# A 4096-cubed matmul with leaky ReLU: the first two output regions computed in three turns over k instead of one

## The chip, the core and the metric

The kernel runs on one core of a Trainium2 chip. The metric is the device time of one launch in microseconds (us). The core has a tensor engine (PE) for matmuls, a vector engine (DVE), a scalar engine (ACT), GpSimd (POOL) and a sync engine (SP). Each engine works through its own list of instructions in order and waits at an instruction until the semaphores that it needs have been raised. POOL and SP also issue DMAs, each into its own queue; both queues are served by the same 16 DMA engines.

## What is computed

```
x = np.matmul(a, b)                 # a, b: 4096 x 4096 fp32
return np.where(x > 0, x, alpha*x)  # alpha = 0.01
```

The products are made in bf16 with fp32 accumulation, so both inputs have to be rounded on the way in, and `a` has to be transposed, because the tensor engine wants k on the partitions for both operands.

## The kernel before

The output is cut into regions of 512 rows by 1024 columns (4 blocks of 128 rows, called mt, times 2 halves of 512 columns, called nt). One region fills all 8 PSUM banks, one bank for each (mt, nt). Two regions, h = 0 and h = 1, lie one under the other and share the same 1024 columns of `b`. The depth k = 4096 is cut into 4 units u of 1024, each of 8 chunks c of 128. A region is 4 x 8 x 4 x 2 = 256 matmuls of 128x128 by 128x512.

**A.** `load_a` (L71 to L85) brings 256 rows of `a` (index mp, two of them for 512 rows) over the k of one unit or half unit. Four DMAs, issued by POOL, read fp32 and write bf16 into an `a16` buffer (there are 4 of these); one DVE transpose (L83) of 32x32 blocks then writes the finished tile into `at`. A DMA on POOL's queue waits for the semaphore of the DMA eight before it, so eight can be under way.

**B.** `load_b` (L87 to L98) brings one chunk: one DMA of 512 KB issued by SP into a `b32` buffer (4 of these), and a cast to bf16 into `bt`, on ACT (L96) for the first 32 chunks and on DVE (L98) for all later ones. The `bt` pool has 6 buffers of one unit each.

**The first two regions** are written out by hand (L168 to L266), because nothing is in SBUF when they start. `subs` (L55) is the list of pieces of k: numbers 0 and 1 are the two halves of unit 0 (4 chunks each, "small"), numbers 2, 3 and 4 are units 1, 2 and 3 (8 chunks each, "large"). `TURNS` (L19) says which pieces are done together before the other region gets its turn. A step is one piece for one region. With one turn holding all five pieces the steps are h0 with pieces 0 to 4, then h1 with pieces 0 to 4: ten steps, numbered 0 to 9.

For each step, L175 to L188 list the loads: for h = 0 two A tiles mixed with the B chunks of the piece, for h = 1 the two A tiles alone, because B is then there already. The loads of step i+1 are put into the engines' lists by `ahead` (L235), in four quarters between the quarters of step i's matmuls. A step that is the last of its turn goes through its matmuls block by block (mt outside, c inside), and behind each block calls `spill(mt)` (L211) and then `ahead(mt)`. Other steps go chunk by chunk (c outside, mt inside). In the last turn `spill` also does the output: two leaky-ReLU instructions on ACT (L232) into an `o` buffer (2 of these) and one DMA to `out`, issued by POOL (L233). So on POOL's list the output DMA of block mt stands ahead of the A loads that `ahead(mt)` adds after it.

During steps 8 and 9 the kernel begins to load the B chunks of the next pair of regions (`issue`, L161; L255 and L263). From region 2 on, a plain loop (L269 to L293) does all 256 matmuls of a region and its output, and the loads are issued one or more units ahead.

Of the kernel before, what the change touches and what calls it, by code (L numbers as in the profile page):

```python
# [15 lines left out]

TURNS = [[0, 1, 2, 3, 4]]  # L19


@with_exitstack
def kernel(
# [76 lines left out]
    def mm(ps, mb, h, pi, u, mt, nt, c, first, last):  # L100
        nc.tensor.matmul(  # L101
            ps,
            at[mb, h, u][:, c, mt * P:(mt + 1) * P],
            bt[pi, u][:, c, nt * NT:(nt + 1) * NT],
            start=first,
            stop=last,
        )

    def new_banks():
        return {  # L110
            (mt, nt): psum_pool.tile([P, NT], FP32, name="ps")
            for mt in range(MT)
            for nt in range(NP)
        }
# [46 lines left out]
    def issue(slot, part):  # L161
# [7 lines left out]
        (t, h, sub, i == len(turn) - 1)  # L169
        for t, turn in enumerate(TURNS)  # L170
        for h in range(HALVES)
# [19 lines left out]
    part = {}  # L191
    if len(TURNS) > 1:
        for piece in queue[0]:
# [3 lines left out]
    for i, (t, h, si, last) in enumerate(steps):  # L197
# [4 lines left out]
        queue[i] = []  # L202
        if si == TURNS[t][0]:
            banks = new_banks()

        def go(mt, c):
            for nt in range(NP):
                mm(banks[mt, nt], 0, h, 0, u, mt, nt, c0 + c, si == TURNS[t][0] and c == 0,
                   last and c == kc - 1)

        def spill(mt):  # L211
            if not last:
                return
            for nt in range(NP):
                ps = banks[mt, nt]
                if len(TURNS) == 1:
                    continue
# [8 lines left out]
                else:  # L226
                    nc.vector.tensor_add(kept, ps, kept)
            if t == len(TURNS) - 1:
                o = o_pool.tile([P, RN], FP32, name="o")
# [99 lines left out]
```

## Time and profile before

| what | value |
|---|---|
| median of 3 runs | 1827.9 us (1827.43 to 1828.4) |
| the profiled execution | 1827.43 us, its span 1825.7 us |
| tensor engine | 8192 matmuls of the product, busy 97% of the span, mean granted clock 0.989 |
| 0 to 165 us (first two regions) | granted clock 0.88 between 12 and 165 us |
| 165 to 1825 us (the other 14) | granted clock 1.00, no idle time of the tensor engine recorded |
| queue of SP (B) | 220.23 MB |
| queue of POOL (A and most of the output) | 98.59 MB, counted as written |

The span is what the profile covers; the 1.7 us between it and the execution's time lie around it. Times inside the trace are counted from the span's start. A row of a timeline gives the start, the duration, the engine, the line and the operation, how many instructions were merged into the row, and in square brackets how long the engine was idle before it and what ended the wait. "DVE at L83" as a releaser means that the transpose of an A tile came last. Some matmul records are missing, so counts of matmuls in a row can be a little low, and the missing ones can be worked out from the order of the program.

### The profile page before, as it was taken

What the parts mean: (1) busy time and instruction counts of PE and PEld (TensorE: products, weight loads), DVE (VectorE), ACT (ScalarE), POOL (GpSimd) and SP (SyncE); (2) the same over time, 40 slices, a digit from 0 to 9 for tenths busy, and PEclk for the clock granted to TensorE, in tenths of its full rate; (3) what the DMA queues carried; (4) which work ended last, traced back from release to release, by engine and by line L of the source; (5) the groups of instructions that cost most, each with busy time, mean ns of one, the idle gap of its engine ahead of it and who ended that gap; (6) DMA issues with size and microseconds to landing.
All of it is one profiled execution on the core that took longest, in us unless ns stands there. A gap on an engine that the chain in (4) does not pass through costs nothing.

```text
span 1825.7 us, 18868 instructions
## 1 busy us (share of the span) xinstructions
PE 1776.4 (97%) x8041; PEld 804.5 (44%) x8204; DVE 475.6 (26%) x465; ACT 174.3 (10%) x290; POOL 253.6 (14%) x448
## 2 busy tenths in 40 slices
PE   5789999999999999999999999999999999999999
PEld 2334444444444444444444444444444444444444
DVE  1454231214442213022452312201255130311000
ACT  5200000000000000000000000000000000000001
POOL 3150000033310000003520000001242000000000
PEclk7899999999999999999999999999999999999999
DMA  9799773465585629155856835617387581644111
GB/s 325 181 162 352 270 272 143 181 141 101 100 235 210 230 105 338 65 196 81 131 100 230 289 126 198 263 64 226 62 111 198 203 337 46 244 171 160 70 46 47
DMA packets 166037, 320.04 MB, mean 175 GB/s; under 512 B 46657, under 2 KB 95809, under 8 KB 165953
## 3 DMA queue, kind: packets, MB, share of 16 engines
q1 hardware_dynamic: 61056, 220.23, 33.0%
q0 software_dynamic: 104896, 98.59, 24.7%
q8 instruction: 64, 1.05, 0.2%
q14 instruction: 21, 0.16, 0.0%
HBM read 285.21 MB, written 67.11 MB: 193 GB/s over the span
## 4 chain that ended last, share of the span: by engine, by line
PE 93%; DMA 4%; issue 2%; POOL 1%; DVE 0%; ACT 0%; POOLq 0%; DVEq 0%
PE ps L101 93%; DMA a<-in_a_dram 4%; POOL a L81 0%; POOL out_dram L233 0%; DVE at L83 0%; ACT o L288 0%; DVEq L83 0%; POOLq L81 0%; POOLq L233 0%; POOLq L310 0%
## 5 line engine op out<-in xcount | busy, mean ns | idle before, releaser
L101 PE MATMUL ps<-bt,at 128*128 128x512 bf16 x8029 | 1772.1, 381 | 43.4 <-DVE at L83 34.7
L101 PEld LDWEIGHTS <-at 128*128 128x128 bf16 x8192 | 803.0, 98 | 1012.5 <-DVE at L83 40.2
L98 DVE CAST bt<-b 128x1024 bf16<-128x1024 f32 x384 | 256.6, 691 | 851.9 <-PE ps L101 553.0
L83 DVE STREAM_TRANSPOSE at<-a 128x2048 bf16<-128x2048 bf16 (+1 forms) x80 | 219.4, 2779 | 365.1 <-DMA a<-in_a_dram 241.9
L288 ACT ACTIVATE o<-ps 128x512 f32<-128x512 f32 x240 | 130.7, 595 | 1524.1 <-PE ps L101 1408.2
L292 POOL DMA_DIRECT2D out_dram<-o x116 | 64.5, 556 | 1364.8 <-ACT o L288 1355.8
L81 POOL DMA_DIRECT2D a<-in_a_dram x320 | 183.4, 587 | 83.4 <-DMA a<-in_a_dram 50.5
L96 ACT CAST bt<-b 128x1024 bf16<-128x1024 f32 x32 | 33.4, 1045 | 26.1 <-DMA b<-in_b_dram 26.1
L232 ACT ACTIVATE o<-ps 128x512 f32<-128x512 f32 x16 | 8.7, 594 | 97.4 <-PE ps L101 87.9
L233 POOL DMA_DIRECT2D out_dram<-o x8 | 5.5, 687 | 66.5 <-ACT o L232 66.5
L126 PE MATMUL ps<-w 128*128 128x512 bf16 x12 | 4.3, 532 | 2.3 <-ACT w L123 2.3
L126 PEld LDWEIGHTS <-w 128*128 128x128 bf16 x12 | 1.5, 131 | 4.6 <-ACT w L123 2.3
L123 ACT ACT_TABLE_LOAD x1 | 1.3, 1283 | 0.7 <-PEq L310 0.7
L122 DVE MEMSET w<- 128x256 uint32 x1 | 0.3, 272 | 0.9 <-PEq L310 0.9
L123 ACT ACTIVATE w<-w 128x8 bf16<-128x8 bf16 x1 | 0.2, 208 | 0.0
L310 POOL MEMSET const-float32-0.0<- 128x1 f32 x1 | 0.1, 98 | 0.2 <-issue 0.2
L310 POOL MEMSET const-bfloat16-1.0<- 128x1 bf16 x1 | 0.1, 101 | 0.0
L310 POOL MEMSET const-float32-1.0<- 128x1 f32 x1 | 0.1, 98 | 0.0
L310 POOL MEMSET const-uint8-127<- 128x1 uint8 x1 | 0.1, 98 | 0.0
## 6 DMA issues: line engine op xcount, KB each, us to landing
b<-in_b_dram SPq DMA_DIRECT2D x416, 512.0 KB, 5.4
out_dram<-o POOLq DMA_DIRECT2D x124, 512.0 KB, 2.9
a<-in_a_dram POOLq DMA_DIRECT2D x192, 128.0 KB, 5.1
a<-in_a_dram POOLq DMA_DIRECT2D x128, 64.0 KB, 3.3
out_dram<-o SPq DMA_DIRECT2D x8, 256.0 KB, 2.0
```

The costliest lines, as they stand in the source:

```text
L81: nc.gpsimd.dma_start(a16[32 * q:32 * q + 32], src.rearrange("(g i) w -> i g w", i=32))
L83: nc.vector.transpose(dst.rearrange("p c (g i) -> p g c i", g=8), a16.rearrange("p g (j c) -> p g c j", c=kc))
L96: nc.scalar.copy(bt[pi, u][:, c0 + c, :], b32)
L98: nc.vector.tensor_copy(bt[pi, u][:, c0 + c, :], b32)
L101: nc.tensor.matmul(ps, at[mb, h, u][:, c, mt * P:(mt + 1) * P], bt[pi, u][:, c, nt * NT:(nt + 1) * NT], start=first, stop=last,)
L123: nc.scalar.activation(w[:, :8], w[:, :8], LRELU, alpha=alpha)
L126: nc.tensor.matmul(wp, w[:, :P], w, start=True, stop=True)
L232: nc.scalar.activation(o[:, nt * NT:(nt + 1) * NT], done, LRELU, alpha=alpha)
L233: nc.gpsimd.dma_start(place(0, h, pairs[0], mt), o)
L288: nc.scalar.activation(o[:, cols], banks[mt, nt], LRELU, alpha=alpha)
L292: nc.gpsimd.dma_start(to, o)
L310: nc = _bacc.Bacc("TRN2", target_bir_lowering=False, num_devices=1)
```

## The change

```
--- before
+++ after
-TURNS = [[0, 1, 2, 3, 4]]
+TURNS = [[0], [1, 2], [3, 4]]
```

The ten steps now are: 0: h0 piece 0; 1: h1 piece 0; 2 and 3: h0 pieces 1 and 2; 4 and 5: h1 pieces 1 and 2; 6 and 7: h0 pieces 3 and 4; 8 and 9: h1 pieces 3 and 4. Steps 0, 1, 3, 5, 7 and 9 are the last of their turn. At each of these all 8 PSUM banks are handed on, so `spill` has work to do, which it skipped with one turn:

```
for nt in range(NP):
    ...
    if h not in part:
        part[h] = bt_pool.tile([P, MT, NP, NT], FP32, name="part", tag="bt")
    kept = part[h][:, mt, nt, :]
    if t == 0:
        if h == 0 and nt:
            nc.vector.tensor_copy(kept, ps)
        else:
            nc.scalar.copy(kept, ps)
    else:
        nc.vector.tensor_add(kept, ps, kept)
if t == len(TURNS) - 1:
    o = o_pool.tile([P, RN], FP32, name="o")
    ...                                   # leaky ReLU now reads kept, not the bank
    nc.gpsimd.dma_start(place(0, h, pairs[0], mt), o)
```

The first turn copies 16 banks to SBUF (12 on ACT, 4 on DVE); the second and third turns add 16 banks each to what is kept there, on DVE; the leaky ReLU of the two regions reads the kept sums. The sums of a region take one buffer of the `bt` pool. The matmuls, their number, the bytes moved and everything from region 2 on stay as they are, apart from which `bt` buffer a unit gets.

## The prediction

> **What bounds the kernel now.** I read the busy shares in 40 slices first. From the fourth slice on PE is busy nine tenths or more at full clock; what can be moved lies in the first 165 us.
>
> ```profile
> PE   5789999999999999999999999999999999999999
> PEclk7899999999999999999999999999999999999999
> ```
>
> Next the timeline of PE in this stretch (the bracket is the wait ahead of the row), and the last of region 2 on ACT's timeline, which dates the end.
>
> ```profile
> 12.20 3.58 PE L101 MATMUL ps<-bt,at 128*128 128x512 bf16 x8 [5.63 <-DVE at L83]
> 18.34 7.90 PE L101 MATMUL ps<-bt,at 128*128 128x512 bf16 x28 [2.56 <-DVE at L83]
> 30.57 0.61 PE L101 MATMUL ps<-bt,at 128*128 128x512 bf16 x1 [4.32 <-DVE at L83]
> ...
> 43.42 1.89 PE L101 MATMUL ps<-bt,at 128*128 128x512 bf16 x4 [3.90 <-DVE at L83]
> 54.50 16.70 PE L101 MATMUL ps<-bt,at 128*128 128x512 bf16 x63 [9.20 <-DVE at L83]
> 72.91 26.94 PE L101 MATMUL ps<-bt,at 128*128 128x512 bf16 x121 [1.71 <-DVE at L83]
> 101.05 1.04 PE L101 MATMUL ps<-bt,at 128*128 128x512 bf16 x4 [1.20 <-DVE at L83]
> 108.22 52.13 PE L101 MATMUL ps<-bt,at 128*128 128x512 bf16 x228 [6.13 <-DVE at L83]
> ```
>
> ```profile
> 209.21 1.08 ACT L288 ACTIVATE o<-ps 128x512 f32<-128x512 f32 x2 [41.33 <-PE ps L101]
> ...
> 219.57 1.08 ACT L288 ACTIVATE o<-ps 128x512 f32<-128x512 f32 x2 [2.37 <-PE ps L101]
> ```
>
> From 209.21 to 219.57 lie 48 matmuls: 0.2158 us each, so a region's 256 take 55.2. Region 2 ended at about 219.5, no wait lies within it, so region 1 ended at 164.2. From 12.2 to 164.2 are 152.0 us for 110.5 of matmuls: 29.1 of waits and 12.4 of matmuls at half clock. Every wait ends with an A tile. DVE's timeline tells when the tiles came:
>
> ```profile
> 17.04 1.25 DVE L83 STREAM_TRANSPOSE at<-a 128x1024 bf16<-128x1024 bf16 x1 [4.89 <-DMA a<-in_a_dram]
> ...
> 39.55 3.81 DVE L83 STREAM_TRANSPOSE at<-a 128x2048 bf16<-128x2048 bf16 x1 [9.04 <-DMA a<-in_a_dram]
> 50.63 3.81 DVE L83 STREAM_TRANSPOSE at<-a 128x2048 bf16<-128x2048 bf16 x1 [7.27 <-DMA a<-in_a_dram]
> 62.45 3.85 DVE L83 STREAM_TRANSPOSE at<-a 128x2048 bf16<-128x2048 bf16 x1 [8.01 <-DMA a<-in_a_dram]
> 69.05 11.24 DVE L83 STREAM_TRANSPOSE at<-a 128x2048 bf16<-128x2048 bf16 x3 [2.75 <-DMA a<-in_a_dram]
> ...
> 99.75 1.25 DVE L83 STREAM_TRANSPOSE at<-a 128x1024 bf16<-128x1024 bf16 x1 [19.45 <-DMA a<-in_a_dram]
> ```
>
> A large tile comes every 11.3 us while B is loading, a small one every 6.1 (the first four transposes start at 10.9, 17.0, 23.9, 29.3). With B gone, 118 to 126 us moved 193 GB/s of A as written, 2.7 us for a large tile's 512 KB. B beside A: ACT casts 15 chunks between 31.35 and 57.25, 1.73 us each. So B takes most of the bandwidth, up to 61 us, and A waits. The second region's tiles fail for another reason:
>
> ```profile
> 94.14 0.55 POOL L233 DMA_DIRECT2D out_dram<-o  x1 [2.88 <-ACT o L232]
> 94.69 2.32 POOL L81 DMA_DIRECT2D a<-in_a_dram  x4
> ...
> 101.10 0.55 POOL L233 DMA_DIRECT2D out_dram<-o  x1 [2.88 <-ACT o L232]
> 101.99 7.99 POOL L81 DMA_DIRECT2D a<-in_a_dram  x14 [0.35 <-issue]
> ```
>
> Their DMAs stand on POOL behind the output DMAs of region 0, which wait for its last matmuls. DMA idles from 80 to 90 us (share 0.01). Issued at 94.69, the tile is there at 99.75.
>
> **The change, step by step.** It moves no byte less. It puts loads in another order, spills 48 banks, and keeps POOL's order "output, then A" in the last turn. I follow the new step order with the durations above.
>
> *Steps 0 and 1.* The first two tiles come as before (10.9, 17.0); step 0 ends at 18.34 + 24 x 0.282 = 25.1. The copies cost ACT 12 x 0.6 (its 128x512 leaky ReLU from PSUM: 595 ns). DVE's 4 copies and 32 adds show nowhere: between 0.60 (that row) and 1.04 (ACT's cast of 128x1024); I take 0.65, near DVE's own 691 ns cast of twice the elements. Step 1's first tile is transposed behind DVE's first copy, which waits for block 0 of step 0 (23.7): 23.7 + 0.65 + 1.25 and semaphores is 25.9, a wait of 0.8. Step 1 ends at 32.8.
>
> *B is held back.* Chunks 5 to 8 fill the four b32 buffers, but their casts stand on ACT behind the copies of step 1's blocks, the first at 30.6. Chunk 9 is issued only when chunk 5 is cast (31.7), lands 5.4 later (page, B's median), 37.3; then every 1.73: chunk 16 at 49.4, chunk 32 at 77.1 instead of 60.7.
>
> *Steps 2 to 5.* Step 2 ends at 40.7, with a stall of some 1 us for casts. Step 3 goes by blocks and its first block needs chunk 16: cast at 50.4, then 48 matmuls, 60.8. Step 4's second tile is transposed behind step 3's last two adds: 60.8 + 1.3 + 1.25, so 63.5; step 4 ends at 69.5, step 5 at 83.3.
>
> *A meanwhile.* Step 3's tiles are issued when transposes free their buffers (26) and land at 31 and 34, almost alone. Then B is back: two small tiles by 44.5, large ones at 55.8, 67.1 and 78.3, and step 6's second at 85.0 (6.7 later, as from 62.45 to 69.05 when B's last chunks went by). Transposed by 88.9, with block 2's adds behind it on DVE: 89.7. So step 6 does four matmuls at 83.3 and waits 5.5 us. Up to here PE could be 5 us later at no cost.
>
> *The half clock.* After the waits of 4.32 and 9.20 us the next 28 and 64 matmuls took 2.9 us more than at full speed; after 6.13 us, 1.6. I charge 2.9. Steps 6 and 7 then end at 89.7 + 124 x 0.2158 + 2.9 + 0.3 for DVE's adds = 119.7.
>
> *Step 8, the costliest.* POOL's list reads: output of block 0, of block 1, first A tile of step 8, outputs of blocks 2 and 3, second tile. DVE's reads: adds of blocks 0 and 1, transpose of the first tile, adds of blocks 2 and 3, transpose of the second. Each is in order, so the two tiles come one after the other. Block 1 of step 7 ends 6.9 before 119.7, at 112.8. Two adds and the leaky ReLU: 114.9. Output issue 0.57: 115.5. The tile lands 5.7 later (5.06 measured above for a small one, 0.5 for the larger size, a little for the outputs): 121.2. Transpose: 125.1. The four adds that stood behind it, 2.6; leaky ReLU 0.6, output issue, semaphores: the second tile is issued at 129.2, lands at 134.9, is transposed by 138.8. The rows bound this landing by 3.3 (page, A's small DMAs) and 11.3 (under B); B's next four chunks sit in their buffers by then, so I stay at the row of 94.69. PE waits from 119.7 to 125.1, does four matmuls, waits to 138.9. Then 124 matmuls and 2.9 of half clock: 168.6. The last two tiles land during step 8.
>
> *After that.* Region 2's B chunks are cast between step 9's adds, some 4 chunks later relative to its start than before; chunk 32 was cast at 182.6 and is needed at 205.8, so 23 us cover that. With that cover gone each late chunk would cost 1.4. The `bt` buffer of the last sums is wanted 27 us into region 2.
>
> *The sum.* 168.6 - 164.2 = +4.4 us. Against the profiled execution's 1827.43: 1831.8. That execution is 0.5 below the median of 1827.9. 0.2%, about what a measurement can tell from no change, is 3.7 us.
>
> **Two rules against rows.** After a wait the matmuls ran at a granted clock of 0.50 from 30.6 to 36 and from 54.5 to 60, about 5.5 us. The Trainium skill ("TensorE: Matmul & The Clock Gate", section "HAM oscillation — how this bites in real kernels") warns of gaps over some 3.4 us, which this change makes too, and the page puts the warm-up at about 3.4 us; by that, as an estimate, each costs 1.7 and the sum would be 1829.4. The rows decide: 2.9.
>
> A large tile under B took 11.3 us. The skill ("DMA: Bandwidth & Descriptors", section "Anatomy of one DMA — SWDGE (gpsimd) path") fits 2.0 us plus bytes over 436 GB/s; by it, as an estimate, a tile of 1 MB read takes 4.4 us, and the two of step 8 would cost 2.6 less, 1829.2. No row here shows a large tile alone from its issue; the small one's 5.06 speaks for the longer value.
>
> **Rivals.**
>
> *Faster: step 6's tiles come sooner.* If A gets more of the DMA than in the old trace, because B now pauses, and the last tile of step 6 lands before 79, the wait of 5.5 and its 2.9 go: 1823.4. For it: 2.7 us alone against 11.3. Against: from 37 us B runs unhindered on ACT (there are no spills there after the first turn), which is the same meeting as from 31 to 61 now. It decides once three large tiles take 9.3 us each or less.
>
> *Faster by much: A always ahead.* Waits only at the start: 12.2 + 110.5 + about 4 of half clock, 127, so 1790. Step 8's order on POOL speaks against it; it would need A's DMAs issued ahead of the outputs.
>
> *Slower by more: step 8's tiles land behind the outputs.* Two outputs of 512 KB precede the second tile, and the L233 DMAs took up to 7.9 us to land. If each tile needs 8.7 instead of 5.7: +6, 1837.8; adds of 1.04 instead of 0.65, eight of them on the path: +3.1, 1834.9.
>
> *No change: the DMA sum decides.* The same bytes, then 1827.4. Against: its idle times differ, none at 80 but a new one before step 8.
>
> **How the numbers follow.** The mechanism as worked out 0.66: 1828 to 1836 (landing 1.5 us shorter twice, to an add of 0.8 and clock), of which 0.42 are above 1831.1 and 0.24 within 0.2%. Slower by more 0.20. Tiles sooner 0.10, of which 0.07 are faster and 0.03 within. Much faster 0.02. No change 0.02. Together faster 0.09, same 0.29, slower 0.62. The range leaves out the much faster case, the lower half of the tiles that come sooner, and the far end of the slow one: 1824 to 1838. The likeliest is 1831.8, given as 1832.
>
> **What would show it.** On PE's timeline a wait of 5 to 6 us near 84, one of about 5 near 120 and one of 12 to 14 behind four matmuls, all ended by the transpose; the first epilogue of region 2 at 213 to 214 instead of 209.21; no cast on ACT between 10 and 30 us; on POOL the A loads of step 8 in two groups some 13 us apart. 16 adds before 92 us and 16 before 170, about 0.65 each. Wrong it would be if step 8's second tile were issued before step 7's end, or if A's large tiles came closer than 9 us while B runs.

## The result: 0.47% slower, and where the time lies

The changed kernel takes 1836.38 us (median of 4 runs, 1836.02 to 1837.16) against 1827.97 us before: a ratio of 1.0047, 95% interval 1.0029 to 1.0064. The profiled execution took 1836.04 us, its span is 1834.3 us, 8.6 more than before. All of it is in the first two regions: the first output instruction of region 2 starts at 217.82 us instead of 209.21, also 8.6 later.

The busy shares in 40 slices of the page, after the change:

```profile
PE   6868999999999999999999999999999999999999
PEclk8878999999999999999999999999999999999999
```

The second slice is better than before (8 instead of 7), the third worse (6 instead of 8), the fourth worse (8 instead of 9): the change wins some time early and gives more of it back later. The timeline of PE, after the change:

```profile
25.90 14.42 PE L101 MATMUL ps<-bt,at 128*128 128x512 bf16 x64 [0.64 <-DVE at L83]
...
50.10 1.01 PE L101 MATMUL ps<-bt,at 128*128 128x512 bf16 x2 [1.01 <-ACT bt L96]
51.78 14.10 PE L101 MATMUL ps<-bt,at 128*128 128x512 bf16 x53 [0.66 <-ACT bt L96]
67.41 20.89 PE L101 MATMUL ps<-bt,at 128*128 128x512 bf16 x94 [1.53 <-DVE at L83]
92.38 29.64 PE L101 MATMUL ps<-bt,at 128*128 128x512 bf16 x122 [4.08 <-DVE part L227]
128.34 1.46 PE L101 MATMUL ps<-bt,at 128*128 128x512 bf16 x3 [6.32 <-DVE at L83]
143.74 81.55 PE L101 MATMUL ps<-bt,at 128*128 128x512 bf16 x359 [13.94 <-DVE at L83]
```

From 26 to 88 us PE has only small waits, the longest 1.89 us; before the change it lost 9.20 us there in one wait alone. Step 6 waits 4.08 us, and step 8 waits twice, 6.32 and 13.94 us, with four matmuls between. Where these two come from shows on the lists of POOL and DVE. POOL's timeline first, after the change:

```profile
117.19 0.55 POOL L233 DMA_DIRECT2D out_dram<-o  x1 [2.88 <-ACT o L232]
117.74 2.34 POOL L81 DMA_DIRECT2D a<-in_a_dram  x4
130.41 0.57 POOL L233 DMA_DIRECT2D out_dram<-o  x1 [10.34 <-ACT o L232]
131.61 0.55 POOL L233 DMA_DIRECT2D out_dram<-o  x1 [0.63 <-ACT o L232]
132.16 5.16 POOL L81 DMA_DIRECT2D a<-in_a_dram  x9
```

Then DVE's, after the change:

```profile
82.34 3.85 DVE L83 STREAM_TRANSPOSE at<-a 128x2048 bf16<-128x2048 bf16 x1 [4.08 <-DMA a<-in_a_dram]
86.10 1.25 DVE L227 TENSOR_TENSOR part<-ps,part 128x512 f32<-128x512 f32 x2
87.99 3.77 DVE L83 STREAM_TRANSPOSE at<-a 128x2048 bf16<-128x2048 bf16 x1 [0.63 <-DMA a<-in_a_dram]
...
124.52 3.76 DVE L83 STREAM_TRANSPOSE at<-a 128x2048 bf16<-128x2048 bf16 x1 [8.29 <-DMA a<-in_a_dram]
128.21 2.44 DVE L227 TENSOR_TENSOR part<-ps,part 128x512 f32<-128x512 f32 x4
139.92 3.77 DVE L83 STREAM_TRANSPOSE at<-a 128x2048 bf16<-128x2048 bf16 x1 [9.27 <-DMA a<-in_a_dram]
```

One reads the two together. The first tile of step 8 is issued at 117.74 behind the output of block 1, is there at 124.5, is transposed by 128.2. Only then come the four sums of blocks 2 and 3, the last of whose matmuls ended at 122.0; the outputs that need them go out at 130.4 and 131.6; the second tile, listed behind them, is issued at 132.16 and transposed from 139.9 to 143.7. PE, which needs it for its fifth matmul of step 8, stands.

### The profile page after: what moved, and what is told of

Its sections match the earlier page's. It is cut to its first block, busy times and chain, and to the rows that moved or that the text cites. A ratio compares the mean times of both kernels' runs of the same rounds, so it can differ in the third digit from the quotient of the medians.

```text
span 1834.3 us, 18947 instructions
## 1 busy us (share of the span) xinstructions
PE 1779.3 (97%) x8041; PEld 805.1 (44%) x8204; DVE 497.7 (27%) x501; ACT 180.8 (10%) x302; POOL 253.6 (14%) x448
## 4 chain that ended last, share of the span: by engine, by line
PE 92%; DMA 4%; issue 3%; POOL 1%; DVE 0%; ACT 0%; DVEq 0%; POOLq 0%
PE ps L101 92%; DMA a<-in_a_dram 4%; POOL a L81 1%; DVE at L83 0%; POOL out_dram L233 0%; ACT o L288 0%; DVEq L83 0%; POOLq L81 0%; DVE part L223 0%; POOLq L233 0%; POOLq L310 0%
## 5 line engine op out<-in xcount | busy, mean ns | idle before, releaser
L288 ACT ACTIVATE o<-ps 128x512 f32<-128x512 f32 x240 | 130.7, 594 | 1524.2 <-PE ps L101 1402.8
L81 POOL DMA_DIRECT2D a<-in_a_dram x320 | 183.7, 588 | 87.8 <-DVE at L83 43.3
L227 DVE TENSOR_TENSOR part<-ps,part 128x512 f32<-128x512 f32 x32 | 20.3, 681 | 41.8 <-PE ps L101 41.8
L232 ACT ACTIVATE o<-part 128x512 f32<-128x512 f32 x16 | 9.5, 628 | 85.7 <-DVE part L227 79.5
L225 ACT COPY part<-ps 128x512 f32<-128x512 f32 x12 | 6.3, 600 | 16.2 <-PE ps L101 16.2
```

The costliest lines, as they stand in the source:

```text
L81: nc.gpsimd.dma_start(a16[32 * q:32 * q + 32], src.rearrange("(g i) w -> i g w", i=32))
L225: nc.scalar.copy(kept, ps)
L232: nc.scalar.activation(o[:, nt * NT:(nt + 1) * NT], done, LRELU, alpha=alpha)
L288: nc.scalar.activation(o[:, cols], banks[mt, nt], LRELU, alpha=alpha)
```

## Experiments

Two theories were to be told apart from each other, and both from a third. The first says that the order on POOL's and DVE's lists at the last hand-over is the loss. The second says that the sums themselves, the handing on of banks through DVE, are it. The third says that the DMA's bandwidth sets the end of region 1 whatever the order.

### The last turn's A tiles ahead of the outputs

```
         elif last:
+            early = h == 0 and t == len(TURNS) - 1
+            if early:
+                for quarter in range(4):
+                    ahead(quarter)
             for mt in range(MT):
                 ...
                 spill(mt)
-                ahead(mt)
+                if not early:
+                    ahead(mt)
```

> The changed kernel, with the two A tiles of step 8 put on the lists of POOL and DVE before step 7's blocks instead of behind the outputs and sums of its blocks 1 and 3. Theory (the order on POOL and DVE costs the waits of 6.3 and 13.9 us of step 8, and the half clock behind them about 2.6): these 22.8 go, 1836.4 becomes about 1814, and region 2's first output comes near 195 us instead of 217.8. Rival (handing banks on through sums on DVE is the cost, wherever the loads stand): at most 3 us better, 1833. Rival (the DMA's bandwidth sets the end of region 1): unchanged, 1835 to 1837.

Measured: 1813.24 us, ratio to the kernel before 0.992 (0.9906 to 0.9935), 23.1 us below the changed kernel; the first output of region 2 starts at 194.96 us. POOL's timeline of this kernel:

```profile
88.03 2.33 POOL L81 DMA_DIRECT2D a<-in_a_dram  x4 [0.38 <-issue]
90.98 2.28 POOL L81 DMA_DIRECT2D a<-in_a_dram  x4 [0.61 <-DVE at L83]
112.75 0.57 POOL L233 DMA_DIRECT2D out_dram<-o  x1 [19.50 <-ACT o L232]
```

Both tiles are issued 20 us ahead of the outputs, and PE's timeline goes through step 8 with no wait:

```profile
91.31 43.55 PE L101 MATMUL ps<-bt,at 128*128 128x512 bf16 x188 [4.01 <-DVE part L227]
136.20 79.17 PE L101 MATMUL ps<-bt,at 128*128 128x512 bf16 x366 [1.35 <-DVE at L83]
```

The first theory holds, in size too. All 48 spills are still there, so they are not the loss by themselves; the same bytes move, so neither is the bandwidth. The edit moves the loads on POOL's list and the transposes on DVE's at once; what the sums add to it shows in the run without them below, and no run moves POOL's list alone.

### The same edit with one turn

The edit above, with `TURNS = [[0, 1, 2, 3, 4]]`.

> One turn, as before the change, with the same edit: the two A tiles of step 5 ahead of the outputs of step 4. Theory: the waits of 1.2 and 6.1 us at 101 to 108 us go, but the tiles of steps 6 and 7 are still issued behind the outputs and give 3 to 6 us of that back as waits of their own: 1822 to 1826. If the turns themselves save anything, the first experiment must end below this one, by 8 us or more. Rival (turns save nothing, the order of loads is all): both end within 3 us of each other.

Measured: 1825.28 us, ratio 0.9985 (0.9976 to 0.9995); the profiled execution took 1827.24. PE's timeline of this kernel, at the hand-over from region 0 to region 1:

```profile
72.88 33.84 PE L101 MATMUL ps<-bt,at 128*128 128x512 bf16 x156 [2.44 <-DVE at L83]
108.13 1.04 PE L101 MATMUL ps<-bt,at 128*128 128x512 bf16 x4 [1.41 <-DVE at L83]
110.88 6.22 PE L101 MATMUL ps<-bt,at 128*128 128x512 bf16 x28 [1.71 <-DVE at L83]
118.17 1.04 PE L101 MATMUL ps<-bt,at 128*128 128x512 bf16 x4 [1.08 <-DVE at L83]
121.84 93.37 PE L101 MATMUL ps<-bt,at 128*128 128x512 bf16 x424 [2.63 <-DVE at L83]
```

The waits of 1.20 and 6.13 us at 101 to 108 are gone, and 6.8 us of shorter ones have come in steps 6 and 7. So with the loads early the turns save 1825.28 - 1813.24 = 12.0 us. They do what they are built for; with the old order of loads that gain is more than lost at their last hand-over.

### No sums

```
                 if t == 0:
                     ...
-                else:
-                    nc.vector.tensor_add(kept, ps, kept)
             ...
-                    done = banks[mt, nt] if len(TURNS) == 1 else part[h][:, mt, nt, :]
+                    done = banks[mt, nt]
```

> The changed kernel without the 32 adds of the second and third turn; the leaky ReLU reads the banks of the last turn, so the outputs of the first two regions lack the sums of the first two turns. Theory: the transposes of steps 4, 6 and 8 no longer stand behind sums; step 4's wait of 1.5 and most of step 6's 4.1 go, and step 8's second tile is issued right behind step 7's end, near 124 instead of 132, which takes 8 of its 13.9 us; some 10 us of waiting in step 8 stay, as the outputs still stand ahead of it on POOL: 1822 to 1827. Rival (the sums are the whole loss): 1814 or lower. Rival (sums cost nothing, all is POOL's order): 1833 to 1836.

Measured: 1825.1 us, ratio 0.9985 (0.9975 to 0.9994). PE's timeline of this kernel:

```profile
52.21 34.22 PE L101 MATMUL ps<-bt,at 128*128 128x512 bf16 x150 [0.70 <-ACT bt L96]
91.86 29.23 PE L101 MATMUL ps<-bt,at 128*128 128x512 bf16 x124 [5.43 <-DVE at L83]
126.49 1.89 PE L101 MATMUL ps<-bt,at 128*128 128x512 bf16 x4 [5.40 <-DVE at L83]
133.45 81.80 PE L101 MATMUL ps<-bt,at 128*128 128x512 bf16 x369 [5.07 <-DVE at L83]
```

Step 8 keeps 10.5 of its 20.3 us of waiting, as expected: the sums take part in the chain by holding the outputs that hold the tile. The time at step 6 was not as expected. Its wait did not go, it grew to 5.43, and its second tile, the first of the three in the last row, came at the same time as with the sums (DVE's timeline of this kernel; the first row is the second small tile, of step 4):

```profile
51.01 1.25 DVE L83 STREAM_TRANSPOSE at<-a 128x1024 bf16<-128x1024 bf16 x1 [4.28 <-DMA a<-in_a_dram]
...
88.04 11.19 DVE L83 STREAM_TRANSPOSE at<-a 128x2048 bf16<-128x2048 bf16 x3 [2.71 <-DMA a<-in_a_dram]
```

### A fifth buffer for A

`a16_pool` with `bufs=5` instead of 4, otherwise the changed kernel.

> The changed kernel with five a16 buffers instead of four. Theory (step 6's second tile was late because POOL sat 10.2 us until step 4's tile was transposed behind step 3's sums and gave its buffer free): the tile lands by 85 instead of 88, step 6 goes on as soon as step 5 is done, its wait of 4 us and some half clock behind it go: 1829 to 1832. Rival (the tile was late for bandwidth, B taking most of it): unchanged, 1835 to 1837.

Measured: 1828.86 us, ratio 1.0004 (0.9994 to 1.0013): 7.5 us below the changed kernel. The size was about as expected, just below the range; the reason was not the one given. POOL still waited 10.0 us for a transpose (61.66 us), while in the run without sums, where POOL had no such wait, the tile came no sooner. What the fifth buffer does is earlier. Two windows of 2 us, the changed kernel (after the length come the busy times of PE, its weight loads, DVE, ACT and POOL with their counts, then the granted clock; the last two columns are the DMA's busy share and GB/s):

```profile
24.00:26.00 2.00, 1.36 (x7) 0.50 (x6) 2.00 (x3) 1.83 (x4) 0.00 (x0) 1.00 0.00 0
26.00:28.00 2.00, 1.95 (x9) 0.89 (x10) 2.00 (x3) 0.38 (x1) 1.86 (x4) 1.00 0.22 17
```

The same windows with five buffers:

```profile
24.00:26.00 2.00, 1.84 (x9) 0.64 (x7) 1.42 (x2) 1.63 (x4) 0.33 (x1) 1.00 1.27 166
26.00:28.00 2.00, 1.52 (x7) 0.70 (x8) 2.00 (x4) 0.42 (x1) 1.28 (x3) 1.00 0.73 95
```

With four, all four A buffers are full and untransposed at 24 us and B is held by ACT's copies, so the DMA stands still. With five, one more tile comes in then, and the later tiles are that much ahead: by the landings of L81's DMAs, step 4's second tile is there at 40.6 us instead of 49.7. Step 6's second tile is transposed from 84.11 instead of 87.99, and PE does not wait for it, only 0.22 us for a sum.

### Step 3 by chunks

```
+            ride = kc - 1 if i == 3 else 0
+            for c in range(ride):
+                for mt in range(MT):
+                    go(mt, c)
             for mt in range(MT):
-                for c in range(kc):
+                for c in range(ride, kc):
```

> The changed kernel, with step 3 done chunk by chunk for its first seven chunks and block by block only for the last, so that PE uses each B chunk for 8 matmuls as it comes, instead of 2. Step 3 then ends near 54 us instead of 66. Theory (step 6 waits for a tile whose landing is set by the bandwidth that B leaves, so what PE wins before is waited away): step 6 still goes on near 92, 1834 to 1837. Rival (PE's lateness of 5 us in step 5, by half clock and waits of two matmuls each, delays the tiles through DVE's order and the a16 buffers): step 6 goes on near 88 or sooner, 1828 to 1832.

Measured: 1836.76 us, ratio 1.0046 (1.0031 to 1.0061). PE's timeline of this kernel:

```profile
25.91 28.16 PE L101 MATMUL ps<-bt,at 128*128 128x512 bf16 x125 [0.64 <-DVE at L83]
...
92.60 29.28 PE L101 MATMUL ps<-bt,at 128*128 128x512 bf16 x122 [9.25 <-DVE part L227]
```

Step 3 ended at 54.1 us instead of 65.9, almost 12 us sooner, and step 6 went on at 92.60 instead of 92.38. Whatever PE wins before the tile of step 6 is waited away. So for the middle steps something of the third theory is left: the tile's time does not hang on PE here (88.21 us against 87.99), nor on the sums in the run without them (88.04), while the DMA engines are at work all the time (330 GB/s on the mean from 34 to 88 us in the changed kernel), and filling a stretch in which they stood still brought the tile forward.

### Two turns

`TURNS = [[0, 1, 2], [3, 4]]`, otherwise the changed kernel.

> Two turns, [[0, 1, 2], [3, 4]], nothing else: the first, small turn is gone and with it 16 of the 48 bank spills, and B runs unbroken over its first 16 chunks while A waits, as before the change. Step 8's order on POOL and DVE stays. Theory (step 8's order is the loss, wherever the turns are cut before it): waits of about 6 and 14 us in step 8 are there again, a wait in step 6 is not, since the second region's first three pieces give A time to come; 1829 to 1833. Rival (many short turns are the loss, fewer are better): 1822 or lower.

Measured: 1828.28 us, ratio 0.9997 (0.9987 to 1.0006), a little below what was expected. PE's timeline of this kernel:

```profile
59.75 54.69 PE L101 MATMUL ps<-bt,at 128*128 128x512 bf16 x247 [1.07 <-DVE at L83]
120.51 1.46 PE L101 MATMUL ps<-bt,at 128*128 128x512 bf16 x3 [6.07 <-DVE at L83]
135.98 69.21 PE L101 MATMUL ps<-bt,at 128*128 128x512 bf16 x302 [14.01 <-DVE at L83]
```

Other turns before it, the same two waits at the last hand-over, to 0.3 us. Step 6 has no wait here; the waits are early instead, as in the kernel before. With this cut the turns gain about as much as the last hand-over costs.

### Other turns, with the loads early

The first experiment's edit, with `TURNS = [[0, 1], [2], [3, 4]]`:

> Turns [[0, 1], [2], [3, 4]] with the last turn's A tiles ahead of the outputs, as in the first experiment. Theory (with step 8's waits gone, what is left is set by how A's tiles and B's chunks share the DMA, and a turn of two small pieces lets A of both regions come before B's large ones): step 6's wait of 4 us shrinks to 1 or 2 and most of step 3's feeding by single chunks goes: 1803 to 1808. Rival (the cut of the turns does not matter once the loads stand early): 1812 to 1815.

Measured: 1806.69 us, ratio 0.9882 (0.9867 to 0.9896), as expected; the longest wait left at step 6 is 1.00 us. And with `TURNS = [[0, 1], [2], [3], [4]]`:

> Turns [[0, 1], [2], [3], [4]], loads early as above: one more hand-over of all banks, 16 more sums. Theory (a hand-over whose next tiles are on the way costs only a few tenths each, and turns of one piece let the second region's tile come while the first works on B as it arrives): at or 1 to 3 us below the kernel with [[0, 1], [2], [3, 4]]: 1801 to 1807. Rival (each hand-over costs its 16 sums of 0.68 us on the way): 5 us or more above it.

Measured: 1801.94 us, ratio 0.9855 (0.984 to 0.987), the best kernel here, 26.7 us below the one before. It has 64 spills and no wait of PE at any hand-over after 57 us; PE's timeline of this kernel:

```profile
34.09 14.42 PE L101 MATMUL ps<-bt,at 128*128 128x512 bf16 x65 [1.07 <-DVE at L83]
...
56.55 148.74 PE L101 MATMUL ps<-bt,at 128*128 128x512 bf16 x665 [0.75 <-ACT bt L96]
```

Sixteen more sums cost nothing that shows; a turn of one piece instead of two gained 4.8 us.

## Why the prediction was right, and what it mis-sized

The direction and the mechanism were right: three waits were named (near 84, of 5 to 6 us; near 120, of about 5; then 12 to 14 behind four matmuls), and 4.08 at 88, 6.32 at 122 and 13.94 at 130 were found. The first of them ended with the sums behind the transpose, as the working had it, not with the transpose. The size was not right: forecast was region 1's end 4.4 us later; measured 8.6, nearly twice that. 1836.4 lies just above the 1828 to 1836 that the prediction gave its own mechanism, and inside the stated range because that also covered a slower rival. In order of the prediction's steps:

- **Steps 0 and 1, B held back: right.** ACT makes no cast between 10.0 and 30.3 us, chunk 9 is cast at 37.66 (37.3 forecast), chunk 16 at 50.68 (49.4). The sums take 681 ns (0.65 taken), the copies on ACT 600.
- **Steps 2 to 5: wrong by 5 us, at no cost.** Step 3 ended at 65.9 instead of 60.8. Fed with one chunk at a time, PE did two matmuls and waited, and the granted clock was 0.50 from 42.8 to 56.4 us, which the step left out. "Up to here PE could be 5 us later at no cost" was borne out by the run with step 3 by chunks.
- **A meanwhile: mis-sized by 2.7 us.** Step 6's second tile was transposed from 87.99, not 85.1, and PE went on at 92.38 instead of 89.7. The term at fault is the two small tiles of step 4, put at 44.5: by the landings of L81's DMAs in the trace they were there at 43.8 and 49.7, so that together they took 14.4 us from step 3's last tile instead of 10.5. The large tiles behind them made some of it good: they landed at 61.2, 72.2 and 82.2 (55.8, 67.1 and 78.3 forecast), and step 6's second at 87.9 (85.0). B's chunks came at 1.85 us each (16 to 32, 50.68 to 80.24), not 1.73, but the tiles were already 5 us late at 49.7, before most of these chunks. The run without sums has the second small tile late in the same way: its transpose starts at 51.01, right behind the DMA. That neither PE, the sums nor POOL's wait for a buffer caused it is shown by the runs without sums and with step 3 by chunks, where the tile came at 88.04 and 88.21. Why the two small tiles took so long beside B stays open. The 11.3 us of a large tile is slightly off too: the two gaps in the old trace are 11.1 and 11.8.
- **The half clock: about right.** 29.64 us for the 124 matmuls that steps 6 and 7 had left is 2.9 above 26.8. Some 2.5 of it are half clock (0.50 from 92.4 to about 97.4); 2.9 had been taken, and 0.3 for sums.
- **Step 8: right in kind, two terms too small.** From issue to the start of the transpose the tiles took 6.8 us (117.74 to 124.52) and 7.8 (132.16 to 139.92); 5.7 was taken for both, from a small tile. That is 3.1 us in all, the largest part of what was missing. In the run without sums both tiles took 6.7 us (115.94 to 122.67 and 122.89 to 129.63), so most of the first 1.1 us seems to be the tile's size; the further 1.0 of the second came where two outputs, a megabyte, had been issued just ahead of it, and was not tested alone. On POOL the two groups of loads are 14.4 us apart (13 forecast).
- **The rest.** Region 2 and all behind it did not move; the later B chunks were covered, as said.

So 2.3 of the missing 4.2 us are in place by the end of step 7 (122.0 instead of 119.7), 2.5 more by the end of step 8's second wait (143.74 instead of 138.9), and 0.6 came back in the last two steps.

On the two rules that were weighed: the half clock after step 6's wait lasted from 92.4 to about 97.4 and cost some 2.5, and after step 8's wait it cost about 2.3 (143.74 to 172.8 us, that is 164.2 and the 8.6, less 26.8). Both are above the 1.7 estimated from the Trainium skill's page "TensorE: Matmul & The Clock Gate", section "HAM oscillation — how this bites in real kernels". The landing of a large tile, 6.8 and 7.8 us, is well above the 4.4 estimated from "DMA: Bandwidth & Descriptors", section "Anatomy of one DMA — SWDGE (gpsimd) path"; the page gives its sum of a fixed part and the bytes per DMA, and here a tile was four DMAs whose issue alone took 2.34 us, behind an output.

The rival of tiles coming sooner did not come about (10.0 to 11.5 us from one large tile's landing to the next while B ran). The rival of no change fell with the result, and the first experiment shows the same bytes in 23 us less. The much faster rival named what was missing, A's DMAs issued ahead of the outputs; with them and other turns the best kernel here reached 1801.9 (1790 in the rival). The slower rival, tiles landing later behind the outputs, came about in part: 6.8 and 7.8 instead of the 8.7 that it named.

## What to carry to other kernels

Where an engine's list is in order, look at what stands ahead of each load, not only at when its data are needed: a load listed behind an output waits for all that the output waits for, and with a transpose on another in-order list behind sums, the delays go one after the other. Handing PSUM banks on through sums in SBUF costs almost nothing while the next tiles are already there; 64 banks are handed on so in the fastest kernel here. And time won ahead of a tile that comes at the DMA's pace is waited away; look instead for stretches where the DMA stands still, such as 24 to 26 us here.

## What was not expected of the hardware

PE fed with two matmuls in every 1.7 us ran at half clock though no single wait was longer than 1.9 us. The granted clock fell at about 42.8 us, within the longest of these waits (1.89 us, up to 43.14). It stayed at 0.50 while PE was fed thinly, and until about 56.4 us, some 4.6 us after the feeding had become full at 51.78. The windows of the changed kernel (the third column from the right is the granted clock):

```profile
40.00:42.00 2.00, 0.91 (x4) 0.23 (x3) 0.47 (x1) 0.61 (x1) 1.15 (x2) 1.00 1.14 367
42.00:44.00 2.00, 0.86 (x2) 0.25 (x2) 0.00 (x0) 1.40 (x2) 0.00 (x0) 0.70 1.18 338
44.00:46.00 2.00, 1.16 (x3) 0.25 (x2) 0.00 (x0) 1.42 (x2) 0.57 (x1) 0.50 1.19 329
54.00:56.00 2.00, 2.00 (x7) 0.60 (x5) 0.00 (x0) 1.09 (x2) 0.00 (x0) 0.50 1.11 348
```

Before the change a wait of 1.71 us at 71 us, after full work, cost no clock at all (1.00 from 70 to 76 us). In the fastest kernel the clock was still 1.00 after a wait of 1.73 us, 0.38 us of work and a wait of 1.86 (up to 53.26 us), and fell at about 54.3. So the length of one wait alone does not decide it. A share of busy time over some microseconds would fit these rows; no run here varies that alone, so it is not shown.
